# Conformer norm: the squares of four tiles and of two later ones summed on GpSimd, the statistic one unit further down

## The chip, the cores and the metric

The kernel runs on one core of one Trainium2 chip. The metric is the device time of one execution in microseconds (us). A core has five engines with a queue each: TensorE (PE in the profile; its weight loads are PEld), VectorE (DVE), ScalarE (ACT), GpSimd (POOL) and SyncE (SP), which here only issues transfers.

## The reference, cut to what matters

A trunk of two layers over 512 positions of width 1024. Layer 0 mixes tokens with a gated DeltaNet, layer 1 with a Conformer convolution; each layer then has a cross-attention into 256 memory positions and a squared-ReLU MLP of width 4096. Every sub-layer begins with an RMS norm. The change sits where the MLP of layer 0 ends and the Conformer of layer 1 begins:

```python
def rms_norm(x, g):
    y = x * lax.rsqrt(jnp.mean(x * x, axis=-1, keepdims=True) + RMS_EPS)
    return y * g

def conformer_conv(h, w_pw1, b_pw1, w_dw, b_dw, ln_g, ln_b, w_pw2, b_pw2):
    u = h @ w_pw1 + b_pw1                                    # 1024 -> 2048
    u = u[..., :D_MODEL] * jax.nn.sigmoid(u[..., D_MODEL:])
    c = causal_depthwise_conv(u, w_dw) + b_dw                # width 31
    c = jax.nn.silu(layer_norm(c, ln_g, ln_b))
    return c @ w_pw2 + b_pw2
...
h = h + sq_relu_mlp(rms_norm(h, mlp_norm[0]), mlp_w_up[0], mlp_w_down[0])
h = h + conformer_conv(rms_norm(h, cv_norm[0]), ...)
```

## The kernel before, in words

Activations lie with channels on the partitions: eight tiles of 128 channels x 512 positions. A matrix product takes three matmuls for each weight block of 128x128, since both operands are split into a high and a low part (`mm3`: high x high at L292, high weight x low activation at L293, low weight x high activation at L294). `Norm.parts` makes the split of one tile `h`: ScalarE writes `xh = g*h`, VectorE writes `xl = g*h - xh`. The products run on these unscaled parts. The factor `rb`, one over the root of the mean square, is multiplied in when a product leaves PSUM.

For `rb`, `Norm.square` lets ScalarE square each tile into `sq` and adds the squares up in `acc`; after the eighth, `split` makes `sqh` (ScalarE) and `sql` (VectorE) of the sum. `Norm.stat` adds over the partitions with two matmuls of ones (`ssq`), takes the root on ScalarE (`sd`) and the reciprocal on VectorE (`rb`).

Weights come in halves of 128x1024, each used by 24 matmuls. SyncE loads one (`raw`), ScalarE casts its high part (`wh`, L251), VectorE, or GpSimd for the later ones, subtracts for the low part (`wl`, L71). Three buffers of `wh` and `wl` rotate, so a cast waits until TensorE has finished with the half three places earlier.

`mlp7(0)` ends with `outs`, which turns the result back into eight tiles `h` and calls `parts` on each: the first four in `outs(range(4))`, the last four in `rest()`. `conformer` then runs the sixteen halves of `w_pw1` in the order of `CONV_SEQ`. Half `hf` of output tile `m` is called unit 2m+hf here. For `m = 0`, `pw_mm` takes the first four channel tiles of unit 0, calls `rest()`, takes the first four of unit 1, and then the second four of both units; the tiles from `rest()` are just being made. `norm.stat` is called inside the end of unit 1. After both halves of a tile `pw_ev(m)` multiplies by `rb` (`sg`, `pa`), applies the sigmoid and starts the convolution of that tile: tile 0 as products on ScalarE (`cvp`) with additions on GpSimd (`ca`), tiles 1 to 4 as multiply-adds on VectorE (`ca`, L1350, the taps), tiles 5 to 7 as matmuls with the tap tiles (`cv`). A LayerNorm (`bn`, `mv`, `cy`), transposes (`lnT`) and `w_pw2` follow.

A scheduler orders the instructions of each engine; each engine then runs its own in that order and waits where an operand is missing.

Of the kernel before, what the change touches and what calls it, by code (L numbers as in the profile page):

```python
# [11 lines left out]
ALU = mybir.AluOpType  # L12
# [25 lines left out]
def tile_trunk(ctx, tc, xT, memT, x_d, mem_d, prm_d, adt_d, bdw_d, tap_d, fin_d, w_ab, w_kq, w_v, w_z, w_dno, w_pw1, w_pw2,  # L38
               w_q, w_k, w_vv, w_o, w_up, w_dn, yT):
    nc = tc.nc  # L40
    pe, act, dve, pool = nc.tensor, nc.scalar, nc.vector, nc.gpsimd
# [14 lines left out]
    def slot(dt=F32, s="u", shape=(P, NT)):  # L56
        return up.tile(list(shape), dt, tag="u", name=nm(s))

    def psum(s="ps"):
        return psp.tile([P, NT], F32, tag="ps", name=nm(s))  # L60
# [9 lines left out]
    def tt(e, o, a, b, op):  # L70
        r = e.tensor_tensor(out=o, in0=a, in1=b, op=op)  # L71
        if e is pool:
            last_pool[:] = [r]
        return r
# [189 lines left out]
    def wnext(key, hf):  # L264
        i = ws["next"]
        assert order[i] == (key, hf), (order[i], key, hf)
        while ws["load"] <= need[min(i + NRAW + 1 + 2 * (order[i][0][0] in ("up", "dn7")), len(order) - 1)]:
            wload()
        while ws["split"] < min(i + (NW if i > 2 else (1, 2, 2)[i]), len(order)):
            wsplit()  # L270
        ws["next"] += 1
        return ws["hl"].pop(i)
# [17 lines left out]
    def mm3(ps, wk, xk, first, last):  # L290
        (wh, wl), (xh, xl) = wk, xk
        pe.matmul(ps, wh, xh, start=first, stop=False)  # L292
        pe.matmul(ps, wh, xl, start=False, stop=False)  # L293
        pe.matmul(ps, wl, xh, start=False, stop=last)  # L294

    def wk(w, k):
        c = slice(k * P, (k + 1) * P)
        return w[0][:, c], w[1][:, c]

    def proj(w, xs, ps, k0=0, k1=KT, inside=None):  # L300
        for k in range(k0, k1):
            mm3(ps, wk(w, k), xs[k], k == 0, k == KT - 1)
            if inside and k in inside:
                inside[k]()
# [24 lines left out]
    def split(src, s):  # L329
        h = slot(F32R, s + "h")  # L330
        act.copy(h, src)  # L331
        lo = slot(F32R, s + "l")
        tt(dve, lo, src, h.bitcast(F32), ALU.subtract)
        return h, lo
# [30 lines left out]
    def root_table():  # L365
        tc.keep_in_program_order(act.activation(small(1), eps_ln, AF.Sqrt))

    class Norm:
        def __init__(self, gname):
            self.g, self.acc, self.xs, self.n = gname, None, [], 0  # L370

        def add(self, t, h):
            self.parts(t, h)
# [6 lines left out]
            pin(stt(xl, h, pc(self.g, t), xh.bitcast(F32), ALU.mult, ALU.subtract))  # L380
            self.xs.append((xh, xl))

        def square(self, h, e=pool):
            sq = slot(s="sq")
            act.activation(sq, h, AF.Square)  # L385
            self.n += 1
            if self.acc is None:
                self.acc = sq
            else:
                tt(dve if self.n == KT else e, self.acc, self.acc, sq, ALU.add)  # L390
            if self.n == KT:
                self.hl = split(self.acc, "sq")

        def stat(self):
# [676 lines left out]
    def mlp7(layer, norm, hres, nxt=None, mid=None):  # L1071
        xs = norm.xs
# [108 lines left out]
        new = [None] * 8  # L1181

        def outs(tiles):
            todo = [(n, c, i) for n in range(2) for c in range(2) for i in tiles]
            pss = {i: psum("hT") for i in tiles}
            for n, c, i in todo:
                j = 2 * n + c
                pe.transpose(pss[i][:, j * P:(j + 1) * P], acc[n, 1 - i // 4, c][:, i % 4 * P:i % 4 * P + P], ident)
            for k, i in enumerate(tiles):
                hn = slot(s="h")  # L1190
                tt(dve, hn, pss[i], hres[i], ALU.add)
                new[i] = hn
                if k:
                    nxt.parts(i - 1, new[i - 1])
            nxt.parts(i, hn)
            if i == 7:
                for hn in new:
                    nxt.square(hn, dve)

        def final(n, m, c):  # L1200
            opens = n not in fin or fin[n][4][c] is None
# [26 lines left out]
        for g in range(4):  # L1228
            ops, us = [{} for _ in range(4)], []
            for i in range(8):  # L1230
                w = wnext(("up", layer, g * 4 + i // 2), i % 2)
# [34 lines left out]
    def conformer(norm, hres, nxt, rest):  # L1266
        xs = norm.xs
        st, xg = {}, {}
# [5 lines left out]
        def pw_mm(m, hf):  # L1274
            w, st[m, hf] = wnext(("pw1", m), hf), psum("pw")
            if m:
                return proj(w, xs, st[m, hf])
            proj(w, xs, st[m, hf], 0, 4)
            if hf == 0:
                st["w"] = w  # L1280
                return rest()
            proj(st.pop("w"), xs, st[0, 0], 4, 8)
            proj(w, xs, st[0, 1], 4, 8, inside={5: norm.stat})

        def pw_ev(m):
            sg = slot(s="sg")
            tt(dve, sg, st.pop((m, 1)), norm.rb, ALU.mult)
            act.activation(sg, sg, AF.Sigmoid, bias=pc("b_pw1", 8 + m))
            a = slot(s="pa")
            tt(dve, a, st.pop((m, 0)), norm.rb, ALU.mult)  # L1290
            if m == 0:
                x4 = c4(wp.tile([P, 544], F32, tag="cv", name=nm("xp"), bufs=NCV))
                pool.memset(x4[:, :, 0:8], 0.0)
                stt(x4[:, :, 8:136], c4(a), pc("b_pw1", m), c4(sg), ALU.add, ALU.mult)
                todo_p.extend(pool_conv(m, x4))
                return
            if m < NTAP:
                x7 = fsp.tile([P, 1024], F32, tag="fs", name=nm("x7"))[:, 0:1008].rearrange("p (q t) -> p q t", q=7)
                pool.memset(x7[:, :, 0:10], 0.0)
                stt(x7[:, 3:7, 8:136], c4(a), pc("b_pw1", m), c4(sg), ALU.add, ALU.mult)  # L1300
                act.copy(x7[:, 0:3, 9:137], x7[:, 4:7, 8:136])
                todo.extend(dve_conv(m, x7))
                return
            x = wp.tile([P, 544], F32, tag="cv", name=nm("xg"), bufs=NCV)
            x4 = c4(x)
            pool.memset(x4[:, :, 0:8], 0.0)
            gl = slot(s="glu")
            stt(gl, a, pc("b_pw1", m), sg, ALU.add, ALU.mult)
            for j in range(4):
                for b in range(4):  # L1310
                    nc.sync.dma_start(out=x4[32 * b:32 * b + 32, j, 8:136],
                                      in_=gl[32 * j:32 * j + 32, 128 * b:128 * b + 128])
            xg[m] = x4
# [4 lines left out]
        def behind(ins, f, *a):  # L1318
            if ins is None:
                return f(*a)  # L1320
            with tc.issue_after(ins.ins):
                return f(*a)
# [55 lines left out]
        def taps_pool(n):  # L1378
            for _ in range(min(len(todo_p), n)):
                todo_p.pop(0)()  # L1380

        def taps_dve(n):
            for _ in range(min(len(todo), n)):
                todo.pop(0)()
# [76 lines left out]
        for i, (kind, u) in enumerate(CONV_SEQ):  # L1461
            if kind == "p":
                m, hf = divmod(u, 2)
                pw_mm(m, hf)
                if hf == 1:
                    pw_ev(m)
            else:
                kv_unit(1, u)

            for ins in gate:  # L1470
                stack.enter_context(tc.issue_after(ins.ins))
            taps_dve(TAPS_U[i])
            stack.close()
            taps_pool(2 if kind == "p" else 1)
            for what, m, *js in after.pop(i, ()):
                {"t": taps, "c": lambda m: conv(m, js), "l": lambda m: ln(), "s": lambda m: root_table(), "o": ln_out, "d": turn,
                 "m": lambda m: behind(first["tap"], moments, m)}[what](m)
                if what == "c":
                    for ins in gate:
                        stack.enter_context(tc.issue_after(ins.ins))  # L1480
                    taps_dve(TAPS_C[m])
                    stack.close()
                taps_pool(3 if what == "c" else 0)
            gate = [x for x in (ws["ins"], mem.get("kf")) if x is not None] if i >= 15 else []
        assert not after
        new = []
        for m in range(8):
            ps = psum("pw2")
            proj(wnext(("pw2", m // 2), m % 2), ss, ps)
            hn = slot(s="h")  # L1490
# [86 lines left out]
    for h in range(8):  # L1577
        uk = max(at["k", h] + 1, T_STAT + 1)
        uq, uv = at["q", h] + 1, at["v", h] + 1
        for u, ev, t, tap, d, key, lag in ((uk, D.ev_k, TAPK.get(h, uk), D.tap_k, D.KT, h, LAG[0]),  # L1580
                                           (uq, D.ev_q, TAPQ.get(h, uq), D.tap_q, D.M, ("q", h), LAG[1]),
                                           (uv, D.ev_v, TAPV[h], D.tap_v, D.VT, h, LAG[2])):
            S.at(u, 4, ev, h)
# [21 lines left out]
    for gq in range(2):  # L1605
# [9 lines left out]
        for i in range(4):  # L1615
            h = 4 * gq + i
# [50 lines left out]
    h = []  # L1667
# [13 lines left out]
    h = xattn(0, n1, h, n2)  # L1681
    n3 = Norm("cv_norm")
    h, rest = mlp7(0, n2, h, n3, lambda: (mem_gain(1, 0), mem_gain(1, 1), taps(NTAP)))
    n4 = Norm("xa_norm1")
    h = conformer(n3, h, n4, rest)
    n5 = Norm("mlp_norm1")
    h = xattn(1, n4, h, n5)
# [38 lines left out]
TAPK = {2: 12, 3: 12}  # L1726
TAPQ = {0: 12}
TAPV = (37, 38, 39, 40, 69, 69, 70, 71)
TAPS_U = (6,) * 16 + (3, 2, 1, 2, 2, 2, 2, 2, 3) + (0,) * 7
TAPS_C = {5: 9, 6: 7, 7: 5}  # L1730
SHARE = 8
# [105 lines left out]
```

## Time and profile before

| what | value |
|---|---|
| median of three runs | 1472.52 us (1470.46 to 1472.95) |
| profiled execution: its own time, its span | 1472.31 us, 1470.6 us |
| granted TensorE clock, mean over the span | 0.998 |
| TensorE, VectorE, ScalarE, GpSimd busy | 99%, 73%, 52%, 18% |

The span is the time between the first and the last instruction; the execution's own time has 1.7 us more around it. TensorE's matmuls are pipelined: a row of 0.39 us can start every 0.23 us. The part of the program in question lies between 800 and 980 us from the start of the span: the tiles of `rest()` are made between 808 and 814 us, and the units of `w_pw1` run until 908 us.

### The profile page before, as it was taken

The page shows a single profiled execution, that of the slowest core. Times are in us where ns is not written, and L with a number is a line of the kernel's source. Part 1 is how long each engine was busy: PE and PEld are TensorE (multiplying, and loading weights), DVE is VectorE, ACT ScalarE, POOL GpSimd, SP SyncE. Part 2 cuts the span into 40 slices and gives each one's busy share as a digit, 9 for nine tenths or more (in the row PEclk, how much of TensorE's full clock was granted, in tenths as well). Part 3 has the DMA queues.
Part 4 walks back from the last instruction along what each step waited for, and adds up shares of the span by engine and source line. Part 5 has one row for each costly group of instructions (what it writes and reads, how often), then busy time and mean ns, then how long its engine had stood idle before and what let it go on. Part 6 is the DMA issues. An engine that isn't in the chain of part 4 may idle for free.

```text
span 1470.6 us, 19621 instructions
## 1 busy us (share of the span) xinstructions
PE 1454.7 (99%) x7298; PEld 1226.6 (83%) x7298; DVE 1068.6 (73%) x1619; ACT 771.8 (52%) x1326; POOL 261.0 (18%) x285
## 2 busy tenths in 40 slices
PE   9999999999999999999999899999999999999998
PEld 7888889988888888888888689988888888888886
DVE  5889889867646766767679799985555766767677
ACT  7765865655434554444354655464444544444354
POOL 1411310103113000000000387302113000000100
PEclk9999999999999999999999999999999999999999
DMA  7232124342213666574766424432204466574853
GB/s 272 94 115 72 58 86 156 131 144 87 73 43 114 158 172 175 142 201 136 203 163 219 151 87 164 171 139 101 72 34 131 138 170 179 138 212 126 232 144 86
DMA packets 62736, 201.83 MB, mean 137 GB/s; under 512 B 7728, under 2 KB 10032, under 8 KB 62640
## 3 DMA queue, kind: packets, MB, share of 16 engines
q1 hardware_dynamic: 52416, 164.39, 31.7%
q0 software_dynamic: 9792, 35.66, 14.0%
q8 instruction: 57, 0.93, 0.2%
q10 hardware_dynamic: 432, 0.52, 0.1%
q14 instruction: 39, 0.32, 0.1%
HBM read 197.66 MB, written 2.10 MB: 136 GB/s over the span
## 4 chain that ended last, share of the span: by engine, by line
PE 92%; DVE 3%; ACT 2%; DMA 1%; issue 1%; SPq 0%; POOL 0%; DVEq 0%; ACTq 0%
PE up L294 8%; PE up L293 8%; PE up L292 8%; PE dn L1123 6%; PE dn L1121 6%; PE dn L1122 6%; PE pw L293 3%; PE pw L294 3%; PE pw L292 3%; PE h L292 2%; PE h L293 2%; PE h L294 2%; PE xo L293 2%; PE q L292 2%; PE q L293 2%; PE q L294 2%
## 5 line engine op out<-in xcount | busy, mean ns | idle before, releaser
L251 ACT CAST wh<-raw 128x1024 fp32r<-128x1024 f32 x259 | 272.0, 1052 | 356.5 <-issue 96.7
L71 DVE TENSOR_TENSOR wl<-raw,wh 128x1024 fp32r<-128x1024 f32 (+1 forms) x250 | 305.7, 1225 | 104.1 <-ACT wh L251 98.2
L292 PE MATMUL up<-xh,wh 128*128 128x512 f32 x512 | 199.7, 390 | 0.0
L294 PE MATMUL up<-xh,wl 128*128 128x512 f32 x512 | 199.3, 389 | 0.0
L293 PE MATMUL up<-xl,wh 128*128 128x512 f32 x512 | 199.2, 389 | 0.0
L293 PEld LDWEIGHTS up<-xl,wh 128*128 128x128 f32 x512 | 96.1, 188 | 20.0
L294 PEld LDWEIGHTS up<-xh,wl 128*128 128x128 f32 x512 | 96.1, 188 | 19.9
L292 PEld LDWEIGHTS up<-xh,wh 128*128 128x128 f32 x512 | 96.1, 188 | 19.8
L239 POOL DMA_DIRECT2D t<-w_dn x48 | 42.2, 917 | 360.9 <-DVE wl L71 239.8
L1121 PE MATMUL dn<-wh,ah 128*128 128x512 f32 x256 | 99.8, 390 | 0.0
L1123 PE MATMUL dn<-wl,ah 128*128 128x512 f32 x256 | 99.6, 389 | 0.0
L1122 PE MATMUL dn<-wh,al 128*128 128x512 f32 x256 | 99.6, 389 | 0.0
L77 DVE SCALAR_TENSOR_TENSOR rl<-up,rb 128x512 f32<-128x512 f32 x64 | 44.2, 690 | 58.2 <-PE up L294 58.2
L1350 DVE SCALAR_TENSOR_TENSOR ca<-x,prm,ca 128x512 f32<-128x512 f32 x112 | 82.3, 754 | 3.6 <-ACT ca L1347 1.3
L251 ACT CAST wh<-t 128x1024 fp32r<-128x1024 f32 x44 | 46.5, 1056 | 55.5 <-PE dn L1122 43.7
L71 DVE TENSOR_TENSOR wl<-t,wh 128x1024 fp32r<-128x1024 f32 x44 | 53.7, 1224 | 29.2 <-ACT wh L251 29.1
L292 PE MATMUL h<-xh,wh 128*128 128x512 f32 x184 | 73.7, 400 | 0.0
L294 PE MATMUL h<-xh,wl 128*128 128x512 f32 x184 | 71.9, 391 | 0.0
L293 PE MATMUL h<-xl,wh 128*128 128x512 f32 x184 | 71.7, 390 | 0.0
L71 DVE TENSOR_TENSOR acc<-acc,dn 128x512 f32<-128x512 f32 x100 | 67.4, 683 | 1.1
L71 POOL TENSOR_TENSOR sq<-sq,sq 128x512 f32<-128x512 f32 x24 | 39.1, 1631 | 147.4 <-ACT sq L385 137.0
L71 DVE TENSOR_TENSOR al<-u,ah 128x512 fp32r<-128x512 f32 x64 | 44.1, 688 | 21.4 <-ACT ah L331 21.4
(385 smaller groups left out, 3567.2 us busy)
## 6 DMA issues: line engine op xcount, KB each, us to landing
raw<-w_dn SPq DMA_DIRECT2D x68, 512.0 KB, 3.6
raw<-w_up SPq DMA_DIRECT2D x64, 512.0 KB, 4.7
t<-w_dn POOLq DMA_DIRECT2D x48, 512.0 KB, 5.7
raw<-w_pw SPq DMA_DIRECT2D x24, 512.0 KB, 3.8
raw<-w_dn POOLq DMA_DIRECT2D x20, 512.0 KB, 5.8
raw<-w_k SPq DMA_DIRECT2D x16, 512.0 KB, 3.4
raw<-w_vv SPq DMA_DIRECT2D x16, 512.0 KB, 4.4
t<-w_dn SPq DMA_DIRECT2D x16, 512.0 KB, 4.4
```

The costliest lines, as they stand in the source:

```text
L71: r = e.tensor_tensor(out=o, in0=a, in1=b, op=op)
L77: return dve.scalar_tensor_tensor(out=o, in0=a, scalar=s, in1=b, op0=op0, op1=op1)
L239: nc.gpsimd.dma_start(out=t, in_=a, accum_op=ALU.add)
L251: ins = [act.copy(h, raw)]
L292: pe.matmul(ps, wh, xh, start=first, stop=False)
L293: pe.matmul(ps, wh, xl, start=False, stop=False)
L294: pe.matmul(ps, wl, xh, start=False, stop=last)
L1121: pe.matmul(ps, xh, w[0][:, s], start=opens and k == 0, stop=False, skip_group_check=True)
L1122: pe.matmul(ps, xl, w[0][:, s], start=False, stop=False, skip_group_check=True)
L1123: pe.matmul(ps, xh, w[1][:, s], start=False, stop=k == 3, skip_group_check=True)
L1350: first["tap"] = dve.scalar_tensor_tensor(out=a, in0=src, scalar=w, in1=a, op0=ALU.mult, op1=ALU.add)
```

## The change

The norm before the Conformer gets a second sum. The squares of the first four tiles are taken at the end of `outs(range(4))` and added on GpSimd. Of the last four tiles, the fifth and the sixth are squared while the seventh and eighth are being made, and their one addition is on GpSimd too, into `side`. The seventh and eighth squares are added on VectorE to the sum of the first four, and then `side` is: three additions on VectorE in place of seven. The statistic is taken inside unit 2 (`STAT = 2`: after its third channel tile) instead of at the end of unit 1, and `pw_ev(0)` is called right behind it.

```diff
@@ class Norm
-            self.g, self.acc, self.xs, self.n = gname, None, [], 0
+            self.g, self.acc, self.xs, self.n, self.side = gname, None, [], 0, None
...
-        def square(self, h, e=pool):
+        def square(self, h, e=pool, side=False):
             sq = slot(s="sq")
             act.activation(sq, h, AF.Square)
             self.n += 1
+            if side:
+                if self.side:
+                    tt(pool, self.side, self.side, sq, ALU.add)
+                self.side = self.side or sq
+                return
             if self.acc is None:
                 self.acc = sq
             else:
                 tt(dve if self.n == KT else e, self.acc, self.acc, sq, ALU.add)
             if self.n == KT:
+                if self.side:
+                    tt(dve, self.acc, self.acc, self.side, ALU.add)
                 self.hl = split(self.acc, "sq")
@@ outs(tiles), in mlp7
                 if k:
                     nxt.parts(i - 1, new[i - 1])
+                if i > 5:
+                    nxt.square(new[i - 2], side=True)
             nxt.parts(i, hn)
-            if i == 7:
-                for hn in new:
-                    nxt.square(hn, dve)
+            for hn in new[0:4] if i == 3 else new[6:8]:
+                nxt.square(hn, pool if i == 3 else dve)
@@ pw_mm, in conformer
             if m:
-                return proj(w, xs, st[m, hf])
+                return proj(w, xs, st[m, hf], inside={STAT: lambda: (norm.stat(), pw_ev(0))} if (m, hf) == (1, 0) else None)
...
-            proj(w, xs, st[0, 1], 4, 8, inside={5: norm.stat})
+            proj(w, xs, st[0, 1], 4, 8)
@@ the loop over CONV_SEQ
-                if hf == 1:
+                if hf == 1 and m:
                     pw_ev(m)
@@ tables
+STAT = 2
```

How the instructions stand. First ScalarE (ACT), from the fourth tile's `xh` on; `h_1568`, `h_1569`, `h_1572` and `h_1575` are the first four tiles. Before:

```order
L378 ACTIVATE xh_1578_7450<-h_1575_7444,prm_73 128x512
L378 ACTIVATE xh_1606_7548<-h_1604_7544,prm_73 128x512
L378 ACTIVATE xh_1609_7554<-h_1605_7546,prm_73 128x512
L378 ACTIVATE xh_1612_7560<-h_1608_7552,prm_73 128x512
L378 ACTIVATE xh_1614_7564<-h_1611_7558,prm_73 128x512
L385 ACTIVATE sq_1616_7568<-h_1568_7430 128x512
```

Now:

```order
L378 ACTIVATE xh_1578_7450<-h_1575_7444,prm_73 128x512
L385 ACTIVATE sq_1580_7454<-h_1568_7430 128x512
L385 ACTIVATE sq_1581_7456<-h_1569_7432 128x512
L385 ACTIVATE sq_1582_7459<-h_1572_7438 128x512
L385 ACTIVATE sq_1583_7462<-h_1575_7444 128x512
L378 ACTIVATE xh_1610_7559<-h_1608_7555,prm_73 128x512
L378 ACTIVATE xh_1613_7565<-h_1609_7557,prm_73 128x512
L385 ACTIVATE sq_1615_7569<-h_1608_7555 128x512
L378 ACTIVATE xh_1617_7573<-h_1612_7563,prm_73 128x512
L385 ACTIVATE sq_1619_7577<-h_1609_7557 128x512
L378 ACTIVATE xh_1620_7580<-h_1616_7571,prm_73 128x512
L385 ACTIVATE sq_1622_7584<-h_1612_7563 128x512
```

Before, all eight squares stood behind the eighth `xh`. Now four stand behind the fourth and two between the last `xh`. The four additions that belong to them stand on GpSimd behind its memsets and ahead of the first `ca`.

Second TensorE (PE), around the statistic. `pw_1628` is unit 1 in both programs; `pw_1640` is unit 2 before, `pw_1632` is unit 2 now. Before:

```order
L294 MATMUL pw_1628_7599<-xh_1614_7564,wl_1587_7477 128x512
L397 MATMUL ssq_1629_7630<-sqh_1624_7591,ones_r_121 128x512
L292 MATMUL pw_1640_7663<-xh_1570_7434,wh_1597_7507 128x512
L397 MATMUL ssq_1629_7630<-sql_1625_7593,ones_r_121 128x512
L293 MATMUL pw_1640_7663<-xl_1571_7436,wh_1597_7507 128x512
```

Now (two matmuls of unit 2 stand further up, among those of units 0 and 1):

```order
L294 MATMUL pw_1628_7599<-xh_1620_7580,wl_1591_7488 128x512
L294 MATMUL pw_1632_7642<-xh_1570_7434,wl_1602_7519 128x512
L292 MATMUL pw_1632_7642<-xh_1573_7440,wh_1601_7518 128x512
L293 MATMUL pw_1632_7642<-xl_1574_7442,wh_1601_7518 128x512
L294 MATMUL pw_1632_7642<-xh_1573_7440,wl_1602_7519 128x512
L292 MATMUL pw_1632_7642<-xh_1576_7446,wh_1601_7518 128x512
L293 MATMUL pw_1632_7642<-xl_1577_7448,wh_1601_7518 128x512
L294 MATMUL pw_1632_7642<-xh_1576_7446,wl_1602_7519 128x512
L292 MATMUL pw_1632_7642<-xh_1578_7450,wh_1601_7518 128x512
L293 MATMUL pw_1632_7642<-xl_1579_7452,wh_1601_7518 128x512
L404 MATMUL ssq_1633_7652<-sqh_1624_7591,ones_r_121 128x512
L294 MATMUL pw_1632_7642<-xh_1578_7450,wl_1602_7519 128x512
```

The first statistic matmul stood right behind the last of unit 1. Now eleven matmuls of unit 2 precede it (these nine and the two further up), and the second follows three places later.

Third ScalarE again, around the sigmoid of tile m=2 (`sg_1672` before, `sg_1670` now). The `cvp` are the products of tile 0's convolution, which GpSimd adds; some are written by two instructions, for two parts of the row. Before:

```order
L251 COPY wh_1678_7868<-raw_1662_7768 128x1024
L1333 ACTIVATE cvp_1675_7859<-xp_1634_7648,prm_73 128x512
L1288 ACTIVATE sg_1672_7844<-sg_1672_7844,prm_73 128x512
L1333 ACTIVATE cvp_1676_7862<-xp_1634_7648,prm_73 128x384
L1335 ACTIVATE cvp_1676_7862<-xp_1634_7648,prm_73 128x128
```

Now:

```order
L251 COPY wh_1676_7861<-raw_1660_7761 128x1024
L1341 ACTIVATE cvp_1673_7851<-xp_1638_7664,prm_73 128x256
L1296 ACTIVATE sg_1670_7836<-sg_1670_7836,prm_73 128x512
L1343 ACTIVATE cvp_1673_7851<-xp_1638_7664,prm_73 128x256
L1341 ACTIVATE cvp_1674_7855<-xp_1638_7664,prm_73 128x128
```

In both programs GpSimd has four `ca` additions at this place, ahead of the `wl` of unit 9. Before, the first of the four had its product complete ahead of the sigmoid. Now the second half of that product stands behind it. Ahead of these, GpSimd had seven `ca` additions and now has five.

## The prediction

> **What bounds the kernel now.** I read the page first, then the list of waits of TensorE over the whole span, then the timeline around its longest wait. In the list the columns after the colon are us in total, times, longest.
>
> ```profile
> PE 1454.7 (99%) x7298; PEld 1226.6 (83%) x7298; DVE 1068.6 (73%) x1619; ACT 771.8 (52%) x1326; POOL 261.0 (18%) x285
> ```
>
> ```profile
> PE ssq L397 <- ACT sqh L331: 4.5, 1, 4.5
> ```
>
> TensorE is busy 99% of the span, and its one long wait is for the Conformer norm's statistic, which this change moves. Columns of a timeline: start, duration, engine, line.
>
> ```profile
> 811.22 0.39 PE L292 MATMUL pw<-xh,wh 128*128 128x512 f32 x1
> ...
> 816.47 0.39 PE L294 MATMUL pw<-xh,wl 128*128 128x512 f32 x1
> 821.39 0.50 PE L397 MATMUL ssq<-sqh,ones_r 128*128 128x512 f32 x1 [4.54 <-ACT sqh L331]
> 822.48 0.79 PE L397 MATMUL ssq<-sql,ones_r 128*128 128x512 f32 x1 [0.21 <-DVE sql L71]
> ...
> 829.36 0.39 PE L292 MATMUL pw<-xh,wh 128*128 128x512 f32 x1
> ```
>
> The granted clock stands third from the end in a row of the windows:
>
> ```profile
> 823.00:826.00 3.00, 3.00 (x10) 2.30 (x9) 1.97 (x1) 1.97 (x2) 0.00 (x0) 0.63 0.58 172
> ```
>
> At 811.22 TensorE begins the second channel half of m=0, at 829.36 the unit m=1, hf=1 ("unit 3"; unit = 2m+hf, 24 matmuls). Between lie 50 matmuls: 24 up to 816.47, two of the statistic, 24 of unit 2. The first 24 start 0.228 apart ((816.47 − 811.22)/23), so 50 need 11.4; they took 18.1. **6.7 us are lost here**: 4.75 waiting, the rest in slow matmuls behind the wait, at a granted clock of 0.63. Why is the sum late?
>
> ```profile
> 812.36 1.63 DVE L77 SCALAR_TENSOR_TENSOR xl<-h,prm,xh 128x512 fp32r<-128x512 f32 x2
> 814.28 4.67 DVE L71 TENSOR_TENSOR sq<-sq,sq 128x512 f32<-128x512 f32 x6 [0.29 <-ACT sq L385]
> 818.87 1.22 DVE L71 TENSOR_TENSOR wl<-raw,wh 128x1024 fp32r<-128x1024 f32 x1
> 820.00 0.69 DVE L71 TENSOR_TENSOR sq<-sq,sq 128x512 f32<-128x512 f32 x1
> 804.90 0.72 ACT L378 ACTIVATE xh<-h,prm 128x512 fp32r<-128x512 f32 x1
> 809.07 1.34 ACT L378 ACTIVATE xh<-h,prm 128x512 fp32r<-128x512 f32 x2 [3.45 <-DVE h L71]
> 812.48 0.73 ACT L378 ACTIVATE xh<-h,prm 128x512 fp32r<-128x512 f32 x1 [0.53 <-DVE h L71]
> 813.11 4.26 ACT L385 ACTIVATE sq<-h 128x512 f32<-128x512 f32 x8
> 817.27 1.98 ACT L251 CAST wh<-raw 128x1024 fp32r<-128x1024 f32 x2
> 820.72 0.62 ACT L331 CAST sqh<-sq 128x512 fp32r<-128x512 f32 x1 [1.47 <-DVE sq L71]
> ```
>
> All eight squares (4.26/8 = 0.53 each) and all seven additions (0.80 apart: five steps and one duration of 0.69 make 4.67) come after the last tile, while ScalarE stood idle 3.45 us before 809.07.
>
> **The change, part by part.** *Squares.* The first four now stand behind the fourth xh: 804.90 + 0.7 + 4 × 0.53 ends near 807.7, inside the idle stretch, so the fifth xh still starts at 809.07. The next two fit in the gaps before the seventh and eighth xh; the last two run 813.1 to 814.2. Cost on the path: nothing. Without that cover each would push xh by 0.53.
>
> *Additions.* Four go to GpSimd, which stood idle for 24.07 us before 832.02, but for memsets before that.
>
> ```profile
> 809.83 0.75 DVE L77 SCALAR_TENSOR_TENSOR xl<-h,prm,xh 128x512 fp32r<-128x512 f32 x1 [0.20 <-ACT xh L378]
> 832.02 4.04 POOL L71 TENSOR_TENSOR ca<-ca,cvp 128x512 f32<-128x512 f32 x3 [24.07 <-ACT cvp L1335]
> 347.39 1.80 POOL L71 TENSOR_TENSOR sq<-sq,sq 128x512 f32<-128x512 f32 x1 [10.32 <-issue]
> 350.06 1.30 POOL L71 TENSOR_TENSOR sq<-sq,sq 128x512 f32<-128x512 f32 x1 [0.87 <-ACT sq L385]
> 347.29 0.75 DVE L77 SCALAR_TENSOR_TENSOR xl<-h,prm,xh 128x512 fp32r<-128x512 f32 x1
> 836.64 3.63 POOL L71 TENSOR_TENSOR ca<-ca,cvp 128x512 f32<-128x512 f32 x2 [0.57 <-ACT cvp L1333]
> 837.34 1.78 DVE L77 SCALAR_TENSOR_TENSOR x<-pa,prm,sg 128x512 f32<-128x512 f32 x1
> ```
>
> At 1.80 each, three from 807.0, when two squares are there, end at 812.4; the side sum, whose second square is ready at 812.5, ends at 814.3. VectorE needs the first at 814.0 and the second at its third addition, 815.6: both are covered. VectorE's three additions end at 814.0 + 3 × 0.80 = 816.4, where seven ended at 820.7. But the two engines hold each other up: beside an xl begun at 347.29 the addition took 1.80, alone 1.30, and an x begun behind a running addition took 1.78. Alone such an instruction takes 0.75, as the xl. Laid over this stage: the first two additions run 807.8 to 810.4, so xl five (809.83 in the row above) begins at 810.4 and ends at 811.1; the third, 811.1 to 812.4, holds six, which ends at 813.0; the side addition, 813.0 to 814.3, holds seven, to 815.0; eight ends at 815.7. TensorE wants them 4, 10, 16 and 22 steps after 811.22, at 812.1, 813.5, 814.9 and 816.2. Only seven is late: **0.2**. Were xl never held, 0; were all four additions to hold it 1.30 each, 813.99 + 5.2 = 819.2, **3.0** late. I take 0.2, because most additions fall beside VectorE's h, which reads PSUM.
> [...]
>
> *The statistic* now stands 35 and 38 matmuls after 811.22 (eleven of unit 2 stand ahead of it), so TensorE arrives at 819.2 and 819.9. On ScalarE two casts still stand before sqh, and each waits for a buffer that TensorE frees:
>
> ```profile
> 828.90 0.39 PE L293 MATMUL pw<-xl,wh 128*128 128x512 f32 x1
> 829.37 1.05 ACT L251 CAST wh<-raw 128x1024 fp32r<-128x1024 f32 x1 [0.50 <-PE pw L293]
> 824.03 3.35 DVE L401 RECIPROCAL rb<-sd 128x512 f32<-128x512 f32 x1 [1.61 <-ACT sd L399]
> 840.38 11.84 DVE L1350 SCALAR_TENSOR_TENSOR ca<-x,prm,ca 128x512 f32<-128x512 f32 x15 [1.27 <-ACT ca L1347]
> ```
>
> A cast starts 0.47 after the last matmul on the buffer starts. That matmul is 22 steps after 811.22, at 816.2, so the casts run 816.7 to 818.7, sqh to 819.3, sql to 820.1. TensorE waits 0.2 and 0.1: **0.3**. Thus the casts, not the sum (816.4), are late next, and the sum has 2.3 us in hand, which also absorbs the 1.7 by which xl eight is later above. With waits this short I expect no slow matmuls. Unit 3 starts at 811.2 + 11.4 + 0.3 + 0.2 = 823.1 instead of 829.36: **6.2 us gained**.
>
> *What follows.* The reciprocal began 1.55 after the second statistic matmul (822.48 to 824.03), so rb is there near 820.1 + 1.55 + 3.35 = 825.0. What VectorE does next ends before it waits again, for the cast behind unit 3: that unit frees its buffer 22 steps after 823.1, so the cast runs 828.6 to 829.6. Then come wl (1.13 from start to start), sg and pa (0.69 each) and x, from 832.2 to 833.0 or 834.0 (0.75 or 1.78), and the first tap 1.3 behind it as at 840.38: at 834.3 to 835.3, so 5.1 to 6.1 earlier, middle 5.6. VectorE thus trails TensorE by 0.6 more than before. Who notices?
>
> ```profile
> 852.85 0.73 ACT L1288 ACTIVATE sg<-sg,prm 128x512 f32<-128x512 f32 x1 [5.47 <-DVE sg L71]
> 854.52 4.12 POOL L71 TENSOR_TENSOR ca<-ca,cvp 128x512 f32<-128x512 f32 x3 [4.04 <-ACT cvp L1335]
> 858.59 4.77 POOL L71 TENSOR_TENSOR wl<-raw,wh 128x1024 fp32r<-128x1024 f32 x2
> 862.45 0.39 PE L294 MATMUL pw<-xh,wl 128*128 128x512 f32 x1
> ```
>
> And by windows (length, then busy us of PE, PEld, DVE, ACT, POOL):
>
> ```profile
> 840.00:880.00 40.00, 40.00 (x180) 33.13 (x179) 38.44 (x54) 23.86 (x42) 32.53 (x22) 1.00 0.29 105
> 880.00:920.00 40.00, 40.00 (x265) 36.38 (x264) 39.15 (x58) 19.77 (x37) 30.71 (x19) 1.00 0.45 154
> 920.00:960.00 40.00, 40.00 (x299) 38.05 (x298) 38.02 (x61) 20.69 (x36) 12.07 (x7) 1.00 0.50 176
> ```
>
> GpSimd's wl of unit 9 is there at 861.0 (858.59 + 4.77/2), used at 862.45: 1.45 in hand. Its additions hang on the sigmoid at 852.85, which hangs on VectorE's taps. Now the second half of one more product stands behind that sigmoid, so four additions, not three, precede the wl: one more of 1.37 (4.12/3), begun some 0.4 sooner, puts it 1.0 later against the sigmoid. 1.45 − 0.6 − 1.0 leaves −0.15; with 5.1 or 6.1 in place of 5.6 it is −0.65 or +0.35: a wait of 0 to 0.65, I take **0.2**. In the LayerNorm stage VectorE must be level again: it was busy 115.6 of 120 us from 840 to 960, so 4.4 are free to take up 0.6: cost nothing; past 4.4, TensorE would wait.
> The weight load that SP now issues ahead of nine tap loads concerns unit 12 and taps of later tiles; one memset that GpSimd now does behind two additions is of a tile filled only behind the sigmoid of m=7: nothing for either.
>
> **Sum**: 6.2 − 0.2 = **6.0**. The profiled execution took 1472.31 (span 1470.6), so 1466.3; it lies 0.2 under the median shown, 1472.52, and the runs shown span 2.5.
>
> **The rivals.**
> *A, collisions (0.13).* All four additions hold xl in full, 3.0 late as above. For it: the 1.78 row. Against: the squares are ready at different times and VectorE's h operations lie between. 6.7 − 0.3 − 3.0 − 0.2 = 3.2 gained: 1469.1.
> *B, GpSimd does not come forward (0.09).* The conv's additions began at 832.02 before; xp comes only about 1 us earlier. If the queue up to unit 9's wl ends no sooner than 861.0, TensorE, 6.2 early, wants it at 856.25 and waits 4.75: 1.4 is left of the gain, 1470.9. For it: GpSimd is busy 32.5 of 40 us there. Against: it idled 4.04 before 854.52, and two fewer additions stand ahead.
> *C, slower (0.05).* Shifted against each other, VectorE and GpSimd collide in the tap stage. VectorE has there, by the grouped view of 840 to 960 (count, busy, mean ns), these instructions with two SBUF inputs:
>
> ```profile
> L71 DVE TENSOR_TENSOR wl<-raw,wh 128x1024 fp32r<-128x1024 f32 x10 | 14.3, 1430 | 1.6 <-ACT wh L251 1.6
> L77 DVE SCALAR_TENSOR_TENSOR x<-pa,prm,sg 128x512 f32<-128x512 f32 x3 | 2.3, 783 | 0.0
> ```
>
> If each of the 13 were held by a whole addition, 1.30, 16.9 would be lost; 4.4 are free and 6.0 were gained, so 6.5 slower: 1478.8. It decides from 10.4 of loss. Against: before, it is some 2 us (means of 1430 and 783 against 1.22 and 0.75).
>
> **How the numbers follow.** Forecast 0.73, A 0.13, B 0.09, C 0.05. The measurement tells apart about 0.2%, 2.9 us; A still counts as faster (3.2 to 3.4 below), B as the same, C as slower: 0.86, 0.09, 0.05. Low end: no wait at all, 6.7 gained, 1465.6, less half the runs' spread, 1464.4. High end: it takes in A, 1469.1, and stops short of B.
>
> **What would show it.** Right: in the list of waits ssq falls from 4.5 to some tenths, the granted clock stays 1.00 after it, unit 3 starts near 823, the first tap near 835. Wrong: pw waiting on xl before the statistic (A), on GpSimd's wl near 856 (B), or lnT on VectorE near 960 with long wl rows (C). Another wait of several us with slow matmuls behind it, at any place, would take the gain back.

## The result and the profile after

The changed kernel takes 1465.14 us (median of 6 runs, 1464.85 to 1466.23) against 1471.47 (6 runs, 1470.46 to 1472.95): a ratio of 0.9958, 95% interval 0.9945 to 0.9970. It is 6.3 us faster. Predicted were 1466.3, within 1464.4 to 1469.1.

The ratio is the time over that of the kernel before. TensorE first: the page's busy shares, and two rows of the list of its waits over the whole span (total, times, longest); the other two are 1.2 at the program's start and 0.2 in the MLP. The 1.0 for `xh` lies at the program's start too, at 8 us.

```profile
PE 1452.9 (99%) x7298; PEld 1225.5 (84%) x7298; DVE 1065.2 (73%) x1615; ACT 771.2 (53%) x1326; POOL 266.8 (18%) x289
```

```profile
PE h L1558 <- ACT xh L378: 1.0, 1, 1.0
PE pw L294 <- POOL wl L71: 0.2, 1, 0.2
```

The 4.5 us on `sqh` have gone from the list. The timeline of TensorE at the places the prediction spoke of (start, duration):

```profile
809.88 0.84 PE L292 MATMUL pw<-xh,wh 128*128 128x512 f32 x3
...
817.91 0.50 PE L404 MATMUL ssq<-sqh,ones_r 128*128 128x512 f32 x1
...
818.71 0.42 PE L404 MATMUL ssq<-sql,ones_r 128*128 128x512 f32 x1
...
821.51 0.39 PE L292 MATMUL pw<-xh,wh 128*128 128x512 f32 x1
...
854.37 0.39 PE L293 MATMUL pw<-xl,wh 128*128 128x512 f32 x1
854.99 0.50 PE L294 MATMUL pw<-xh,wl 128*128 128x512 f32 x1 [0.23 <-POOL wl L71]
...
958.54 1.35 PE L1453 MATMUL lnT<-ident,cy 128*128 128x128 f32 x8
...
1455.61 0.39 PE L1130 MATMUL dn<-wl,ah 128*128 128x512 f32 x1
```

The granted clock behind the statistic, third from the end of a row of the windows, is 1.00, where it was 0.63:

```profile
818.00:821.00 3.00, 3.00 (x13) 2.37 (x14) 2.82 (x3) 0.69 (x1) 0.00 (x0) 1.00 0.56 182
```

**Read such a pair from an anchor.** The second half of m=0 begins at 809.88 here and at 811.22 before: 1.34 us of difference lie ahead of every changed instruction. In all runs below this start lies between 809.40 and 811.74, though up to the first early squares, near 804, the programs do the same work. So two executions are compared from this point on. From it to unit 3 it is 821.51 − 809.88 = 11.63 us, where it was 18.14: 6.51 gained. The last two anchors before were these:

```profile
965.86 1.35 PE L1445 MATMUL lnT<-ident,cy 128*128 128x128 f32 x8
...
1462.88 0.39 PE L1123 MATMUL dn<-wl,ah 128*128 128x512 f32 x1
```

To the LayerNorm's transposes the gain is 154.64 − 148.66 = 5.98, to the last matmul 651.66 − 645.73 = **5.93**. This last stretch, from the start of the second half of m=0 to the last matmul, is called "the stretch" below. The two profiled executions lie 7.17 apart (1472.31, 1465.14), the medians 6.33.

The other engines, VectorE, ScalarE and GpSimd, at the rows shown of before:

```profile
808.47 1.02 DVE L77 SCALAR_TENSOR_TENSOR xl<-h,prm,xh 128x512 fp32r<-128x512 f32 x1 [0.20 <-ACT xh L378]
...
810.02 1.18 DVE L77 SCALAR_TENSOR_TENSOR xl<-h,prm,xh 128x512 fp32r<-128x512 f32 x1
...
811.73 2.24 DVE L77 SCALAR_TENSOR_TENSOR xl<-h,prm,xh 128x512 fp32r<-128x512 f32 x2
813.88 2.27 DVE L71 TENSOR_TENSOR sq<-sq,sq 128x512 f32<-128x512 f32 x3
...
819.90 3.35 DVE L408 RECIPROCAL rb<-sd 128x512 f32<-128x512 f32 x1 [0.18 <-ACT sd L406]
...
832.96 11.84 DVE L1358 SCALAR_TENSOR_TENSOR ca<-x,prm,ca 128x512 f32<-128x512 f32 x15 [1.51 <-ACT ca L1355]
```

```profile
804.16 2.18 ACT L385 ACTIVATE sq<-h 128x512 f32<-128x512 f32 x4
807.71 1.34 ACT L378 ACTIVATE xh<-h,prm 128x512 fp32r<-128x512 f32 x2 [1.37 <-DVE h L71]
...
815.34 2.01 ACT L251 CAST wh<-raw 128x1024 fp32r<-128x1024 f32 x2 [1.73 <-issue]
817.25 0.61 ACT L331 CAST sqh<-sq 128x512 fp32r<-128x512 f32 x1
```

```profile
805.58 3.36 POOL L71 TENSOR_TENSOR sq<-sq,sq 128x512 f32<-128x512 f32 x2
...
809.02 1.63 POOL L71 TENSOR_TENSOR sq<-sq,sq 128x512 f32<-128x512 f32 x1
811.45 1.30 POOL L71 TENSOR_TENSOR sq<-sq,sq 128x512 f32<-128x512 f32 x1 [0.80 <-ACT sq L385]
...
829.61 1.30 POOL L71 TENSOR_TENSOR ca<-ca,cvp 128x512 f32<-128x512 f32 x1 [16.86 <-ACT cvp L1343]
...
846.69 5.89 POOL L71 TENSOR_TENSOR ca<-ca,cvp 128x512 f32<-128x512 f32 x4 [5.25 <-ACT cvp L1343]
852.54 4.76 POOL L71 TENSOR_TENSOR wl<-raw,wh 128x1024 fp32r<-128x1024 f32 x2
```

The four early squares lie inside ScalarE's idle stretch, of which 1.37 us are left. The sum ends at 813.88 + 2.27 = 816.15, but `sqh` starts at 817.25, right behind two casts: the sum has 1.1 us in hand.

### The profile page after: what moved, and what is told of

Same layout as the page of the kernel before. It is cut to its first block, busy times and chain, and to the rows that moved or that the text cites. A ratio compares the mean times of both kernels' runs of the same rounds, so it can differ in the third digit from the quotient of the medians.

```text
span 1463.4 us, 19623 instructions
## 1 busy us (share of the span) xinstructions
PE 1452.9 (99%) x7298; PEld 1225.5 (84%) x7298; DVE 1065.2 (73%) x1615; ACT 771.2 (53%) x1326; POOL 266.8 (18%) x289
## 4 chain that ended last, share of the span: by engine, by line
PE 94%; DVE 3%; ACT 2%; DMA 1%; issue 0%; POOL 0%; SPq 0%; POOLq 0%; DVEq 0%
PE up L292 8%; PE up L294 8%; PE up L293 8%; PE dn L1130 6%; PE dn L1128 6%; PE dn L1129 6%; PE pw L294 3%; PE pw L292 3%; PE pw L293 3%; PE h L292 3%; PE h L293 3%; PE h L294 3%; PE xo L293 2%; PE xo L294 2%; PE q L292 2%; PE q L293 2%
## 5 line engine op out<-in xcount | busy, mean ns | idle before, releaser
L71 POOL TENSOR_TENSOR sq<-sq,sq 128x512 f32<-128x512 f32 x28 | 45.4, 1621 | 148.3 <-ACT sq L385 134.2
```

## The experiments

**1. The statistic alone moved, 2. the squares alone.** The first leaves all squares and additions at the end:

```diff
-                if i > 5:
-                    nxt.square(new[i - 2], side=True)
...
-            for hn in new[0:4] if i == 3 else new[6:8]:
-                nxt.square(hn, pool if i == 3 else dve)
+            if i == 7:
+                for hn in new:
+                    nxt.square(hn, dve)
```

> The statistic is moved as in the change, all eight squares and seven additions stay at the end on ScalarE and VectorE as before. All times here on the clock of the changed kernel's trace, in which the second half of m=0 begins at 809.88. The scheduler of this program puts the two matmuls of the statistic 44 and 49 places behind that, further down than in the changed kernel (35 and 38), so TensorE arrives at 819.9 and 821.0. The seventh addition ends where it did before, 820.69 - 1.35 = 819.3, sqh at 820.0; sql stands behind one more wl, at 821.2. My theory (it is the wait that counts, whichever side closes it): waits of 0.1 and 0.2 to 0.4, no slow matmuls, but the reciprocal then stands behind a wl and ends near 827.2 instead of 823.3; xp is 3 us and the first tap 1.2 us later than in the changed kernel, unit 9's wl on GpSimd too. 1465.1 + 0.2 + 1.2 = 1466.5, range 1465.5 to 1467.5: four fifths of the gain. Rival 1, the early sum carries the gain: the wait stays above 2 us with slow matmuls behind it, 1468 to 1469. Rival 2, the place alone carries all and the late reciprocal costs nothing: 1465.1.

The second keeps these lines of the change and puts the statistic back:

```diff
-                return proj(w, xs, st[m, hf], inside={STAT: ...} if (m, hf) == (1, 0) else None)
+                return proj(w, xs, st[m, hf])
...
-            proj(w, xs, st[0, 1], 4, 8)
+            proj(w, xs, st[0, 1], 4, 8, inside={5: norm.stat})
...
-                if hf == 1 and m:
+                if hf == 1:
```

> The squares and additions are as in the change, the statistic stays at the end of unit 1 as before. TensorE arrives at the statistic at 816.85 - 1.35 = 815.5 on the clock of the changed kernel's trace. My theory (the two casts ahead of sqh on ScalarE gate it, not the sum): sqh is no earlier than in the changed kernel, 817.86, so TensorE waits 2.4 and 0.1, and some slow matmuls follow, 0 to 1.0 (the wait of 4.5 before cost 1.95 of them). 1465.1 + 2.2 + 0 to 1.0 = 1467.3 to 1468.3, I take 1467.8. Rival, the early sum is what counts and sqh follows it at 816.15: wait 1.3, no slow matmuls, 1466.0. Rival, nothing is gained without the move: 1471.5.

Measured: 1469.03 us (ratio 0.9981, 0.9972 to 0.9990) and 1468.84 (0.9982, 0.9973 to 0.9991). Each half brings some two fifths of the gain. The statistic alone, rows of TensorE, VectorE, ScalarE and GpSimd:

```profile
820.17 0.50 PE L404 MATMUL ssq<-sqh,ones_r 128*128 128x512 f32 x1 [0.20 <-ACT sqh L331]
858.06 0.50 PE L294 MATMUL pw<-xh,wl 128*128 128x512 f32 x1 [2.90 <-POOL wl L71]
...
823.90 3.35 DVE L408 RECIPROCAL rb<-sd 128x512 f32<-128x512 f32 x1
...
821.68 1.05 ACT L251 CAST wh<-raw 128x1024 fp32r<-128x1024 f32 x1 [1.56 <-DMA raw<-w_pw]
822.63 0.69 ACT L406 ACTIVATE sd<-ssq,eps_rms 128x512 f32<-128x512 f32 x1
...
828.45 1.28 ACT L1295 ACT_TABLE_LOAD   x1
829.74 0.72 ACT L1295 ACTIVATE sg<-sg,prm 128x512 f32<-128x512 f32 x1
...
836.09 11.84 DVE L1357 SCALAR_TENSOR_TENSOR ca<-x,prm,ca 128x512 f32<-128x512 f32 x15 [1.26 <-ACT ca L1354]
...
832.98 1.29 POOL L71 TENSOR_TENSOR ca<-ca,cvp 128x512 f32<-128x512 f32 x1 [26.25 <-ACT cvp L1342]
```

The wait at the statistic shrank to 0.2 as expected, so moving it is enough to close that gap. The wait came back elsewhere: the root `sd` stood behind a cast that waited for its weights, the reciprocal behind a `wl`; `rb` ended at 827.25 instead of 823.25, the conv's first addition on GpSimd began at 832.98 instead of 829.61, and unit 9's `wl` was 2.9 late. The time lies 1.5 above the range I gave. The end of `rb` is not what I missed: 827.2 was expected. I had priced what follows at 1.2, and the first tap came 3.0 later than in the changed kernel (836.09 against 832.96, 0.13 of it ahead of the anchor). VectorE's product for the first sigmoid ended at 827.97, but ScalarE did a cast first (from 827.37) and then loaded the table for the sigmoid (`ACT_TABLE_LOAD`, 1.28), so the sigmoid began at 829.74. In the changed kernel this load ran at 822.60, and ScalarE still waited 1.08 for the product behind it. The first rival came near the time but named the wrong place. Stretch 648.69.

The squares alone, TensorE and ScalarE:

```profile
813.36 0.50 PE L293 MATMUL pw<-xl,wh 128*128 128x512 f32 x1
...
817.90 0.50 PE L404 MATMUL ssq<-sqh,ones_r 128*128 128x512 f32 x1 [1.95 <-ACT sqh L331]
...
817.23 0.61 ACT L331 CAST sqh<-sq 128x512 fp32r<-128x512 f32 x1
```

`sqh` starts at 817.23, as in the changed kernel at 817.25, although TensorE now comes for it two microseconds sooner. The early sum does not bring `sqh` forward beyond the casts, as expected. The wait is 1.95, not 2.4, and the time is 0.5 above the range I gave. Here TensorE also waits for an `xl`, which the list does not show: the matmul at 813.36 starts 0.52 behind the one before it, so 0.3 is lost. In the changed kernel the matmul in its place starts at 813.51, behind two of unit 2 that the scheduler put further up, and loses nothing. Stretch 647.86. So the early sum buys the time of `rb`, the later place buys the wait that the casts would leave.

**3. Without the second sum.** The last four squares stay at the end, with four additions on VectorE:

```diff
-                if i > 5:
-                    nxt.square(new[i - 2], side=True)
...
-            for hn in new[0:4] if i == 3 else new[6:8]:
+            for hn in new[0:4] if i == 3 else new[4:8]:
```

> Only the first four squares are taken early and summed on GpSimd; the last four are squared and added at the end, four additions on VectorE in place of three, no second sum. The scheduler puts the statistic 37 and 45 places behind 809.88, at 818.3 and 820.1. The sum ends 0.7 later, at 816.9; the casts end at 817.3. My theory (the casts gate sqh, and the sum has 1.1 us in hand): sqh still at 817.9, no wait of TensorE at all; sql behind a second wl at 819.5, in time; the reciprocal 1.3 us later than in the changed kernel. With one addition fewer on GpSimd beside it, xl is held less. 1465.1 within 0.5. Rival, the sum gates: sqh at 817.6 + 0.6, the wait grows by 0.5 or more and the time to 1466 or above.

1466.25 us (0.9959, 0.9946 to 0.9971); stretch 645.54, 0.2 shorter than the changed kernel's. Timeline of TensorE and ScalarE (the anchor is at 810.82 here, 0.94 later):

```profile
819.21 0.40 PE L404 MATMUL ssq<-sqh,ones_r 128*128 128x512 f32 x1
...
817.74 0.61 ACT L331 CAST sqh<-sq 128x512 fp32r<-128x512 f32 x1
```

TensorE waits for nothing at the statistic. `sqh` again stands right behind the casts, which ran 0.45 earlier than expected; an addition more on VectorE, which ended the sum at 817.28, did not delay it. The median lies 0.65 above the range I gave, in that of the rival, but the rival's wait is not there, and the stretch is no longer than the changed kernel's. Nothing in the trace shows that the second sum is needed; why the median is 1.1 above the changed kernel's stays open.

**4. GpSimd's additions doubled**, to delay the sum past the casts:

```diff
                     tt(pool, self.side, self.side, sq, ALU.add)
+                    tt(pool, self.side, self.side, sq, ALU.add)
...
                 tt(dve if self.n == KT else e, self.acc, self.acc, sq, ALU.add)
+                if twice:
+                    tt(e, self.acc, self.acc, sq, ALU.add)
...
-                nxt.square(hn, pool if i == 3 else dve)
+                nxt.square(hn, pool if i == 3 else dve, twice=i == 3)
```

> Each of the four additions on GpSimd is done twice (these squares count twice in the statistic, so the norm is another number). The order on TensorE is that of the changed kernel. GpSimd then needs 6 x 1.6 from 805.6 to 815.2 and two more to 818.0; VectorE's third addition ends at 818.7, past the casts (817.3), and gates sqh: 819.4, 1.5 later than in the changed kernel. My theory: TensorE waits 1.6 to 2.0 for the statistic, xl of the last tiles is held more often (0 to 1.0 us more of waiting on xl), slow matmuls 0 to 0.7: 1466.6 to 1468.3, I take 1467.2. [...] Rival A of the prediction (xl held in full): pw waits on xl for 3 us or more ahead of the statistic, 1469 to 1470. Rival, GpSimd has more cover than that: 1465.1.

1469.58 us (0.9985, 0.9977 to 0.9994), 1.3 above the expected range. TensorE, VectorE and ScalarE:

```profile
820.27 0.72 PE L407 MATMUL ssq<-sqh,ones_r 128*128 128x512 f32 x1 [2.74 <-ACT sqh L331]
...
811.25 2.89 DVE L77 SCALAR_TENSOR_TENSOR xl<-h,prm,xh 128x512 fp32r<-128x512 f32 x2
815.32 4.24 DVE L71 TENSOR_TENSOR sq<-sq,sq 128x512 f32<-128x512 f32 x3 [1.19 <-POOL sq L71]
...
819.60 0.62 ACT L331 CAST sqh<-sq 128x512 fp32r<-128x512 f32 x1 [2.73 <-DVE sq L71]
```

Now the sum gates `sqh`, and the cover of 1.1 us is gone. TensorE still waits for no `xl`. What I had sized too low are the wait (2.74, expected 1.6 to 2.0) and the slow matmuls behind it, about which more below. Stretch 650.13.

**5. The same four additions on VectorE** (`pool` replaced by `dve` at both places):

> As the changed kernel, but the four additions on GpSimd are done on VectorE, at their places; the order on TensorE and ScalarE stays. The three of the first tiles come at 806.4 to 808.7 by the changed kernel's clock (third square at 806.3, 0.75 each), between a wl and the fifth h, which then starts 1.7 later; the fifth xh is there at 810.1 where TensorE wants it at 809.9, the seventh xl at 814.1 where it wants it at 813.8. My theory: no xl is held any more (0.75 each instead of 1.02 to 1.49), but 0.5 to 0.7 of new waits of TensorE on xh or xl; the statistic is not earlier, since the casts gate sqh at 817.3: 1465.7, stretch from the second half of m=0 to the last matmul 0.3 to 0.8 longer than the 645.73 of the changed kernel. Rival (the collisions with GpSimd cost the changed kernel something on the path): 1464.9 and a shorter stretch.

1465.43 us (0.9952, 0.9939 to 0.9964), stretch 645.94. Every `xl` takes its 0.75 again:

```profile
806.88 2.28 DVE L71 TENSOR_TENSOR sq<-sq,sq 128x512 f32<-128x512 f32 x3
...
810.55 0.75 DVE L77 SCALAR_TENSOR_TENSOR xl<-h,prm,xh 128x512 fp32r<-128x512 f32 x1 [0.19 <-ACT xh L378]
811.82 0.74 DVE L77 SCALAR_TENSOR_TENSOR xl<-h,prm,xh 128x512 fp32r<-128x512 f32 x1
```

So the 1.02, 1.18 and 2.24 of the changed kernel were GpSimd's doing, and nothing on the path hung on them: without them the stretch is 0.2 longer, not shorter. The three additions at 806.88 now hold up the fifth `h`, which starts at 809.07, but the new waits of 0.5 to 0.7 that I expected from it are not in the list. That the additions stand on GpSimd is not what made the kernel faster; that they are early is.

**6. The statistic later still** (`STAT = 6`), **7. unit 9's `wl` on VectorE**, on top of experiment 3:

```diff
-        gp = kind == "pw1" and 2 * i + hf > 6 or j and kind == "K" and i == 1 and hf == 0
+        gp = kind == "pw1" and 2 * i + hf > 6 and 2 * i + hf != 9 or j and kind == "K" and i == 1 and hf == 0
```

> As the changed kernel, with the statistic after the seventh channel tile of unit 2 (STAT = 6), 46 and 47 places behind 809.88 instead of 35 and 38. My theory: TensorE arrives at 820.4 and waits for nothing there; the reciprocal ends 2 us later than in the changed kernel, at 825.2, xp 2 us later, but VectorE and ScalarE have to wait for the cast behind unit 3 (to 828.0) anyway, so the first tap moves by 0 to 0.5 and unit 9's wl on GpSimd still makes TensorE wait 0.2 to 0.7. Stretch from the second half of m=0 to the last matmul 645.4 to 646.0 against 645.73: no change that can be measured, 1465.1. Rival (a reciprocal that ends later reaches unit 9's wl in full, as with the squares left at the end): wait there 2 us, 1467.0.

> As the kernel without the second sum (its stretch from the second half of m=0 to the last matmul was 645.54 us, with one wait of 0.23 on unit 9's wl, at which 0.4 was lost), but unit 9's wl is done on VectorE instead of GpSimd. My theory: that wait goes, VectorE does 1.2 us more between the taps and has room for it before the LayerNorm: stretch 645.1 to 645.3, 0.4 less, too little for the times to show: 1465 to 1466. Rival: VectorE, busy 98% there, passes the 1.2 us on to the LayerNorm and TensorE waits at lnT or at another wl: stretch 646 or above.

1465.47 us (0.9954, 0.9942 to 0.9967) and 1465.52 (0.9952, 0.9938 to 0.9965); stretches 645.95 and 645.37. With the later statistic TensorE waits for nothing there and longer for unit 9's `wl`; what is saved at one end is lost at the other. `rb` ends 1.6 later than in the changed kernel, counted from the anchor, but the first tap is only 0.2 later: the table load (821.97) still runs before the sigmoid's operand is there. In experiment 1 `rb` was 3.9 later and the load was in the way. The wait here:

```profile
854.75 0.50 PE L294 MATMUL pw<-xh,wl 128*128 128x512 f32 x1 [0.66 <-POOL wl L71]
```

With that `wl` on VectorE the wait is gone, but the stretch is only 0.17 shorter than in experiment 3, less than half of what I expected: a later matmul on a `wl` of GpSimd now starts 0.50 behind the one before it (878.23, 878.73). No variant beats the changed kernel by anything that can be measured: the shortest stretch is 0.36 under its own.

**8 to 12. The clock behind a wait.** Experiment 4 once more, experiments 1 and 2 twice more each:

> The kernel with the doubled GpSimd additions once more (the statistic counts those squares twice). There TensorE waited 2.74 for the statistic and ran at a granted clock of 0.50 for some 3 us behind it; yet behind a wait of 2.90 on unit 9's wl, in the kernel with the statistic alone moved, it stayed at 1.00. [...] If the length of the wait decides, 0.50 again.

> The kernel with the statistic alone moved, once more, for the clock. So far each slow stretch (granted clock 0.50) lasted 3.4 us: from 821.82 to 825.22 before, 820.38 to 823.78 and 821.46 to 824.87 in the two runs with the doubled additions, worked out from the granted clock of 1 us windows. It began 2.2 to 5.0 us after TensorE fell idle, and a wait of 2.90 in this kernel had none. [...] If it is something in the program that decides, 1.00 and 648.7 again.

> The same kernel a third time, same two cases: clock 1.00 behind the wait of 2.9 and 648.7, or one slow stretch of 3.4 us and 650.2 to 650.5. [...]

> The kernel with the early squares and the statistic at its old place, once more, for the clock. The wait of 1.95 had a clock of 1.00 behind it and 647.86 us from the second half of m=0 to the last matmul. [...] If waits under some length never slow it: 1.00.

> The same kernel a third time: mostly 1.00 and 647.9; 649.5 in the rarer case.

| kernel | wait | slow stretch behind it, us | stretch |
|---|---|---|---|
| additions doubled, 1st, 2nd | 2.74, 2.75 | 3.4, 3.4 | 650.13, 649.84 |
| statistic alone, 1st, 2nd, 3rd | 2.90, 2.89, 2.89 | none, 3.4, 6.8 | 648.69, 650.27, 651.50 |
| squares alone, 1st, 2nd, 3rd | 1.95, 1.95, 1.95 | none, 3.4, none | 647.86, 649.57, 647.92 |

Experiments 8 to 12 are one execution each: 1470.56, 1471.00, 1471.51, 1471.12 and 1468.86 us. The same kernel with the same wait comes with and without slow matmuls. The first executions ran on another chip than the later ones, but the second and third of the squares alone ran on one chip and differ, so the chip does not decide it. Two slow stretches in a row were in none of the expectations; that one would be the rarer case behind a wait of 1.95 was an estimate of mine, for which three runs are too few. How the length is read: in windows of 1 us the granted clock is 0.5 or 1, and in between where it changes. The third run of the statistic alone:

```profile
857.00:858.00 1.00, 0.00 (x0) 0.00 (x0) 0.96 (x2) 0.00 (x0) 1.00 (x1) 0.94 0.00 0
858.00:859.00 1.00, 0.33 (x1) 0.34 (x2) 0.96 (x3) 0.00 (x0) 1.00 (x2) 0.50 0.00 0
...
864.00:865.00 1.00, 1.00 (x5) 0.81 (x3) 1.00 (x3) 0.17 (x1) 1.00 (x2) 0.65 0.05 16
```

0.94 means 0.12 us at half speed, 0.65 means 0.70: slow from 857.88 to 864.70, 6.8 us. In the kernel before it was 0.18 of this window and 0.22 of that, 821.82 to 825.22, 3.4 us:

```profile
821.00:822.00 1.00, 0.60 (x2) 0.30 (x2) 1.00 (x2) 0.34 (x1) 0.00 (x0) 0.91 0.81 279
...
825.00:826.00 1.00, 1.00 (x5) 0.76 (x5) 1.00 (x1) 0.30 (x1) 0.00 (x0) 0.89 0.09 37
```

So not the length of a wait alone decides whether the clock falls. One slow stretch cost 1.6 to 1.7 us (650.27 against 648.69, 649.57 against 647.86), two 2.8.

## Why the prediction was right

- **What is lost, 6.7 us:** right. Of the 18.14 − 11.4 lost, 11.63 − 11.4 = 0.23 are left, so 6.51 came back. Near 2 us of the loss were slow matmuls, and only one execution of the kernel before was traced: that each of its executions has them is not shown.
- **Squares, cost nothing:** right; the fifth `xh` still waits 1.37 for its `h`, not for a square.
- **Additions:** 1.68, 1.63 and 1.30 each, not 1.80 throughout. The four `xl` were held by 0.27 + 0.44 + 0.61 = 1.3 us in all, predicted 1.7 for the eighth, and no matmul waited: 0 instead of 0.2, the lower of the two bounds. Experiment 5 shows that the holding is real, and experiment 2 that in another order on TensorE it costs 0.3; so the 0 hangs on where the scheduler put two matmuls of unit 2. The 0.2 let each `xl` begin only when the addition beside it ended; no row shows that. The rows show these holds, on an `xl` of 0.75, so VectorE waits here, and not only GpSimd as in the rows at 347 (1.80 for an addition of 1.30); and the `h` beside additions (809.42, 811.12) took 0.68, as with GpSimd idle (810.50 and 811.76 before); what spares it is not shown.
- **The casts gate `sqh`:** right, and shown by both sides: with the sum as it is, `sqh` comes at 817.23 or 817.25 whether TensorE arrives early or late (experiment 2); only a sum that ends past the casts moves it (experiment 4). No run puts `sqh` ahead of the casts. On the clock of before `sqh` was to end at 819.3; it ended at 817.86 + 1.34 = 819.2.
- **The wait left at the statistic, 0.3:** 0.23 lost in all, most of it around the first of the two matmuls, whose start lies 0.32 behind the one before it and 0.33 ahead of the next. No slow matmuls: right.
- **Unit 3, 6.2 earlier:** 6.51, since the 0.2 for `xl` and a tenth of the 0.3 did not come.
- **First tap 5.1 to 6.1 earlier:** 840.38 − 832.96 − 1.34 = 6.08, the early end. The bound was the right one: `x` took 0.78, as without a collision.
- **Unit 9's `wl`, a wait of 0.2:** the wait is 0.23. TensorE's matmuls there start 0.62 apart instead of 0.23, so it cost 0.4: a wait is priced by the gap between starts, not by the wait that the list gives. That the forecast hit is partly luck. The sigmoid came 852.85 − 845.42 − 1.34 = 6.1 earlier, 0.5 more than the middle I took; TensorE came 6.5 earlier, 0.3 more than I took; and the `wl` began 852.54 − 845.42 = 7.12 behind the sigmoid, where it was 858.59 − 852.85 = 5.74: 1.4 later, not 1.0. The three errors nearly cancel.
- **LayerNorm stage, nothing:** right, the gain is 5.98 at `lnT` and 5.93 at the last matmul.
- **The sum:** 6.0 predicted, 5.93 in the stretch, again by errors that cancel: 0.3 more was gained up to unit 3, and 0.4 more was lost behind it. That 1465.14 came out 1.2 under 1466.3 is not the change's doing: 1.34 of the two profiles' difference lies ahead of it.

Of the rivals, A fell at the size of each hold, 0.27 to 0.61 instead of 1.30: the additions had run for a part of their time beside an `h`, 1.00 us where the sixth `xl` began (809.02 to 810.02) and 0.28 at the seventh (811.45 to 811.73). B fell at GpSimd's queue: it idled 5.25 us ahead of the additions there, and its `wl` pair came forward from 858.59 to 852.54, 4.7 from the anchor, where 6.5 − 1.45 = 5.05 would have left no wait. C fell as VectorE's `wl` of the tap stage took less, not more; the grouped view of 833.6 to 953.6, against 1430 ns:

```profile
L71 DVE TENSOR_TENSOR wl<-raw,wh 128x1024 fp32r<-128x1024 f32 x10 | 13.1, 1314 | 2.6 <-ACT wh L251 2.6
```

The three `x` there took a little more, 864 ns each against 783; the 112 taps, which C leaves out, took 752 against 754.

## What to carry to other kernels

A reduction that one engine waits for has two handles: begin its sum while the operands still come, and put its consumer further down among work that needs nothing from it; here either one alone brought two fifths, because the next lateness (the casts, or the reciprocal's users on GpSimd) took over. Before moving such a step, follow its result to the last engine that uses it: with the sum left late the wait came back 38 us later, on a weight split behind GpSimd's additions. And price a wait by the gap between starts, not by its length in the list; behind waits of 1.95 and of 2.90 us the same program ran here with and without a slow stretch, and one of 3.4 us cost 1.6 to 1.7.

## What the runs showed of the hardware

- The clock falls to half (0.50 granted) for 3.4 us at a time, or for 6.8, and not in every execution of one and the same program: behind 1.95 us of waiting in one of three runs, behind 2.7 in two of two, behind 2.9 in two of three, and behind 4.5 in the one trace of the kernel before. What decides is not shown. Waits of 0.2 to 0.7 had none: 1.00 from 818 to 824 around the 0.20 of experiment 1, and from 854 to 860 around the 0.66 of experiment 6. Kernels with a wait of 2 to 4.5 us also spread more from run to run (2.6 to 3.8 us between extremes, in 11 to 27 runs) than those without (0.6 to 1.9, in 5 or 6); that the clock causes this is only argued, and more runs alone widen such a spread.
- Between executions of programs that are alike up to there, the start of the second half of m=0 moved by up to 2.3 us. Where it was read, nearly all of it is there in the first 47 us: the first `dt` matmul of layer 0 starts at 45.09 in experiment 4, whose second half of m=0 starts at 809.40, and at 46.82 in the kernel before (811.22). What causes it stays open.
